# The chunk recurrence of an S5 layer as a hardware tensor scan in a rotated frame, with its rotation table built on GpSimd

## The chip, the core and the metric

The kernel runs on one core of one Trainium2 chip. The core has TensorE (PE, matrix products; PEld loads its weights), VectorE (DVE), ScalarE (ACT), GpSimd (POOL) and SyncE (SP), which run their own instruction queues in order and meet through semaphores; SP, and here POOL too, also issue the DMA transfers. The metric is the device time of one execution in microseconds (us), the median of several runs. A difference of 0.2% is about what a measurement of this kernel can tell from no change.

## The reference, cut to what matters

One inference step of a two-layer decoder: layer 0 mixes tokens with HGRN2, layer 1 with S5, and each layer then has a SwiGLU block and a per-layer embedding. There are 512 prompt tokens and 64 sample tokens (8 sequences of 8), 1024 features, all in 32-bit floats. The S5 mixer is the part that changes:

```python
u = x.astype(f32).reshape(bsz, t, S5_GROUPS, S5_GROUP)          # 64 groups of 16 channels
lam_bar = jnp.exp(lam * delta)                                  # 64 groups x 64 complex states
bu = jnp.einsum('btgc,gpc->btgp', u.astype(jnp.complex64), b_bar)
bu = bu.at[:, 0].add(lam_bar * h0)
_, h = lax.associative_scan(s5_combine, (a_el, bu), axis=1)     # h_t = lam_bar * h_{t-1} + bu_t
y = jnp.einsum('btgp,gcp->btgc', h, c_mat).real + d_skip * u
y = jax.nn.gelu(y.reshape(bsz, t, D_MODEL))
val, gate = jnp.split(y @ w_glu, 2, axis=-1)
return val * jax.nn.sigmoid(gate), h_last.real, h_last.imag
```

## The kernel before

The 576 tokens lie in two blocks of 288 columns. For S5 each block is 36 chunks of 8 tokens: block 0 holds prompt chunks 0 to 27 and the 8 sample chunks, block 1 prompt chunks 28 to 63. Within a chunk everything is a matrix product; from chunk to chunk a complex recurrence runs, `h[k+1] = lam8 * h[k] + z[k]`, for 64 groups by 64 states. A state's real part lies on partitions 0 to 63 and its imaginary part on 64 to 127, so one step of the recurrence (`advance`, L1428) is five VectorE operations: one product, two products that swap the halves (64 partitions each), two sums.

The S5 layer in program order:

1. While layer 0's SwiGLU runs on TensorE, a generator (`s5_prep`, `s5_prep_steps`) computes the layer's coefficient matrices in small steps on VectorE, and sends them to DRAM scratch through POOL's DMA queue (`zw_scratch`, `cl_scratch`, `mg_scratch`). It goes round 18 times; the `zw` tile has a single buffer.
2. `z_part` of block 0: TensorE makes the chunk inputs z, eight groups (an octet) at a time; ScalarE copies them from PSUM into the state tile `HS[0]` (in the trace a tile with the name `xl`).
3. The chunk recurrence of block 0 on VectorE: `many` joins neighbouring chunks in pairs (wide operations), `pair_step` runs the recurrence over the pairs with `lam16` (64-column operations, one chunk pair after the other), `many` fills in the chunks between.
4. `z_part` of block 1 (into `HS[1]`), then `lag_part` for eight octets (the products inside a chunk, for both blocks), then `out_part(0, o)` for eight octets: TensorE applies the output matrices to the states, VectorE adds the result to `u` (the eight `u<-u,mm` operations), ScalarE applies Gelu, and SP sends `y` to DRAM and reads it back as features (`y_load`). The recurrence of block 1 (`last_states`) is a generator whose steps are placed between these octets by the tables `SL` and `SO0`; what is left of it comes later.
5. The GLU products of block 0 for three output tiles, then `out_part(1, o)`, which needs all states of block 1, then the other GLU products.

ScalarE and VectorE take PSUM banks in turn: TensorE has four banks (`mm`) for all of these products, so it goes on only when one has been read.

The weights stream through all of this: each 512 KB slot is loaded raw (`wraw`, two buffers), rounded by ScalarE (`whi`), and the rest is subtracted (`wlo`). During the S5 part that subtraction runs on POOL, otherwise on VectorE.

Of the kernel before, what the change touches and what calls it, by code (L numbers as in the profile page):

```python
# [8 lines left out]
FP32 = mybir.dt.float32  # L9
# [4 lines left out]
OP = mybir.AluOpType  # L14
# [54 lines left out]
OCT = 2  # L69
SL = (0, 1, 1, 1, 1, 1, 1, 0)  # L70
SO0 = (1, 1, 1, 1, 2, 1, 1, 1)
SY0 = (1, 1, 1, 1, 1, 1, 1, 1)
SE = 1
# [69 lines left out]
def hybrid_decoder_kernel(ctx: ExitStack, tc: tile.TileContext, a: dict):  # L143
# [984 lines left out]
    lam8 = const.tile([128, 2, NG], FP32, name="lam8")  # L1128
    lam16 = const.tile([128, 2, NG], FP32, name="lam16")
    ZL = const.tile([128, NG, 9], FP32, name="zl")  # L1130
# [5 lines left out]
    def s5_prep_steps(sp):  # L1136
# [37 lines left out]
        yield  # L1174
        t1 = s64("t1")
        for j in range(2, 9):
# [133 lines left out]

        todo = []
        for i in range(18):
            if 0 < i < 8:
                zeros(i)
            if i < 16:
                load(i)
                yield
            if i >= 2:
                lag_kernels(i - 2)
                if (i - 2) % 8 == 7:  # L1320
                    todo += [((i - 2) // 8, s, j) for s in range(8) for j in range(4)]
                yield
            if 0 < i < 17:
                coeffs(i - 1)
                yield
                inputs(i - 1)
                yield
            for _ in range(4):
                if todo:
                    toeplitz(*todo.pop(0))  # L1330
        while todo:
            toeplitz(*todo.pop(0))
            if len(todo) % 4 == 0:
                yield
# [51 lines left out]
    def z_part(blk, o, zw):  # L1386
# [3 lines left out]
        if blk == 0:  # L1390
            copy(HS[0][:, g, 1:KA], v[:, :, 0:KA - 1])
            copy(HS[1][:, g, 0:1], v[:, :, KA - 1:KA])
# [55 lines left out]

    def many(blk, x0, n, half):

        gs = slice(32 * half, 32 * half + 32)
        w = [t[:, 0:32 * n].rearrange("p (g n) -> p g n", n=n) for t in s5["work"]]
        x, y = (HS[blk][:, gs, i:i + 2 * n - 1:2] for i in (x0, x0 + 1))
        advance(y, x, y, n, w, gs=gs)

    def pair_step(j):
        advance(chunk_state(j + 2), chunk_state(j), chunk_state(j + 2), lam=lam16)

    s5 = {}

    def layer0_to_1():
# [32 lines left out]


        spare = {}
        chunk_tiles("xh", spare, 1)
        spare = spare[1].rearrange("p g k -> p (g k)")
        s5["work"] = [spare[:, T * i:T * i + T] for i in range(2)]
        settle(0)  # L1500
        for b in range(2):
            chunk_tiles("xl", HS, b)
        nc.vector.memset(HS[0][:, :, 0:1], 0.0)


# [52 lines left out]
        def last_states():  # L1558
            for half in range(2):
                many(1, 0, 18, half)  # L1560
                yield
            for j in range(KA - 1, 63, 2):
                pair_step(j)
                if j == KA - 1:
                    advance(chunk_state(KA), chunk_state(j), chunk_state(KA))
                yield
            advance(po, chunk_state(63), ZL[:, :, 8])
            nc.vector.tensor_scalar(po, po, NSG, None, op0=OP.mult)
            nc.gpsimd.dma_start(a["s5o"], po)
            for half in range(2):  # L1570
                many(1, 1, 17, half)
                yield

# [10 lines left out]
        yt = [[spare[:, (4 + o % 4) * NB:(5 + o % 4) * NB] for o in range(8)],  # L1584
              [U[0][:, 8 * o:8 * o + 8].rearrange("p g k -> p (g k)") for o in range(8)]]
        for o in range(8):
# [16 lines left out]
        for o in range(8 - YD, 8):  # L1603
            step(y_loads[0, o])
        tails["scan"] = scan

# [214 lines left out]
```

## Time and profile before

| | before |
|---|---|
| median of 3 runs | 1597.84 us (1597.0 to 1600.13) |
| profiled execution: its own time, its span | 1600.95 us, 1599.1 us |
| mean granted TensorE clock | 0.98 |
| busy: PE, DVE, ACT, POOL | 95%, 59%, 43%, 15% of the span |

All times of the trace are counted from the start of the profiled span. The span is 1.85 us shorter than that execution's own time, and the profiled execution is 3.1 us slower than the median run. TensorE is busy nearly everywhere; its share is low in one place, between about 900 and 1050 us, which is the S5 mixer.

### The profile page before, as it was taken

How to read it: one execution, taken by the hardware profiler on the slowest of the kernel's cores; microseconds unless marked ns; L12 is line 12 of the kernel's file. 1: busy time of each engine (PE TensorE's matmuls, PEld its weight loads, DVE VectorE, ACT ScalarE, POOL GpSimd, SP SyncE). 2: the span in 40 equal slices, each digit the busy share in tenths (PEclk: the TensorE clock that was granted, in tenths of full speed). 3: DMA queues.
4: the chain of work that ended last, by engine and by line, in shares of the span. 5: the costliest groups of instructions: out<-in, count | busy, mean ns of one | idle time of the engine just before them, and what ended most of it. 6: DMA issues, size and time to landing. Idle time of an engine off the chain costs nothing.

```text
span 1599.1 us, 30007 instructions
## 1 busy us (share of the span) xinstructions
PE 1516.2 (95%) x12550; PEld 1468.0 (92%) x12550; DVE 940.2 (59%) x1833; ACT 687.7 (43%) x1159; POOL 238.6 (15%) x284
## 2 busy tenths in 40 slices
PE   8999999889999999999999956799999999999998
PEld 8898989788999999999989956799999999999997
DVE  5748475858557666743486799457533333334685
ACT  5646464736532233123377533336522232133375
POOL 1303020202001112260012432202000000000111
PEclk9999999999999999999999997899999999999999
DMA  5213131242225666753216973332222222223021
GB/s 184 96 67 108 68 109 68 83 126 93 67 70 145 194 191 182 213 153 94 79 67 197 166 280 83 88 106 80 67 80 93 80 80 80 92 80 119 28 79 59
DMA packets 96390, 175.59 MB, mean 110 GB/s; under 512 B 41792, under 2 KB 56816, under 8 KB 96256
## 3 DMA queue, kind: packets, MB, share of 16 engines
q1 hardware_dynamic: 87856, 149.56, 30.7%
q0 software_dynamic: 8400, 24.13, 5.5%
q8 instruction: 98, 1.61, 0.4%
q14 instruction: 36, 0.29, 0.1%
HBM read 148.72 MB, written 24.94 MB: 109 GB/s over the span
## 4 chain that ended last, share of the span: by engine, by line
PE 76%; DVE 14%; ACT 5%; DMA 2%; issue 2%; POOL 1%; SPq 0%; DVEq 0%; ACTq 0%; POOLq 0%
PE mm L299 24%; PE mm L300 23%; PE mm L301 23%; DVE xh L203 2%; DVE wlo L203 1%; DVE xl L203 1%; DVE am L203 1%; DVE b L580 1%; DVE ac L203 1%; DVE xf L203 1%; PE mm L1377 1%; PE tr L709 1%; ACT whi L200 1%; DVE ln_z L203 1%; DVE ln_q L203 1%
## 5 line engine op out<-in xcount | busy, mean ns | idle before, releaser
L299 PE MATMUL mm<-xh,whi 128*128 128x288 f32 x2048 | 611.1, 298 | 7.6 <-ACT xh L200 4.0
L300 PE MATMUL mm<-xl,whi 128*128 128x288 f32 x2048 | 610.2, 298 | 4.5 <-POOL xl L203 3.0
L301 PE MATMUL mm<-xh,wlo 128*128 128x288 f32 x2048 | 607.6, 297 | 1.3 <-DVE wlo L203 1.3
L299 PEld LDWEIGHTS mm<-xh,whi 128*128 128x128 f32 x2048 | 389.0, 190 | 14.0 <-ACT xh L200 5.6
L300 PEld LDWEIGHTS mm<-xl,whi 128*128 128x128 f32 x2048 | 388.9, 190 | 8.1 <-POOL xl L203 4.6
L301 PEld LDWEIGHTS mm<-xh,wlo 128*128 128x128 f32 x2048 | 388.8, 190 | 1.5 <-DVE wlo L203 1.5
L200 ACT ACTIVATE whi<-wraw 128x1024 fp32r<-128x1024 f32 x208 | 218.6, 1053 | 223.1 <-PE mm L300 122.4
L203 DVE TENSOR_TENSOR wlo<-wraw,whi 128x1024 fp32r<-128x1024 f32 x200 | 246.1, 1247 | 29.3 <-ACT whi L200 28.7
L299 PE MATMUL mm<-hhi,whi 128*128 128x288 f32 x704 | 209.6, 298 | 0.0
L301 PE MATMUL mm<-hhi,wlo 128*128 128x288 f32 x704 | 207.8, 295 | 0.0
L300 PE MATMUL mm<-hlo,whi 128*128 128x288 f32 x704 | 207.5, 295 | 0.0
L203 DVE TENSOR_TENSOR fs<-fs,mm 128x288 f32<-128x288 f32 x88 | 40.0, 454 | 267.3 <-PE mm L301 258.2
L299 PEld LDWEIGHTS mm<-hhi,whi 128*128 128x128 f32 x704 | 132.3, 188 | 1.7 <-issue 1.4
L300 PEld LDWEIGHTS mm<-hlo,whi 128*128 128x128 f32 x704 | 132.3, 188 | 0.3
L301 PEld LDWEIGHTS mm<-hhi,wlo 128*128 128x128 f32 x704 | 132.2, 188 | 0.0
L299 PE MATMUL mm<-xhi,whi 128*128 128x320 f32 (+1 forms) x384 | 121.7, 317 | 0.0
L300 PE MATMUL mm<-xlo,whi 128*128 128x320 f32 (+1 forms) x384 | 113.6, 296 | 0.0
L301 PE MATMUL mm<-xhi,wlo 128*128 128x320 f32 (+1 forms) x384 | 113.5, 295 | 0.0
L203 POOL TENSOR_TENSOR ln_s<-ln_s,xf 128x288 f32<-128x288 f32 x24 | 24.3, 1010 | 576.5 <-DVE xf L203 454.9
L200 ACT ACTIVATE hhi<-fs 128x288 fp32r<-128x288 f32 x88 | 38.9, 442 | 149.3 <-DVE fs L203 149.3
L197 ACT ACTIVATE fs<-mm,eps 128x288 f32<-128x288 f32 x88 | 44.1, 501 | 136.0 <-PE mm L301 135.8
L299 PEld LDWEIGHTS mm<-xhi,whi 128*128 128x128 f32 x384 | 72.8, 190 | 6.9 <-issue 4.4
(292 smaller groups left out, 2159.9 us busy)
## 6 DMA issues: line engine op xcount, KB each, us to landing
wraw<-in_w_dram SPq DMA_DIRECT2D x198, 512.0 KB
wraw<-in_w_dram POOLq DMA_DIRECT2D x10, 512.0 KB, 5.2
S<-in_s_dram SPq DMA_DIRECT2D x8, 512.0 KB
out_hgs_dram<-So SPq DMA_DIRECT2D x8, 512.0 KB
wr<-wt_scratch SPq DMA_DIRECT2D x16, 256.0 KB
bT<-in_s5bt_dram SPq DMA_DIRECT2D x16, 256.0 KB
cl_scratch<-cl POOLq DMA_DIRECT2D x16, 256.0 KB, 3.2
zw_scratch<-zw POOLq DMA_DIRECT2D x16, 256.0 KB, 6.2
```

Of the source, the lines that this page charges most:

```text
L197: nc.scalar.activation(out, in_, func, bias=ZERO if bias is None else bias, scale=scale)
L200: nc.scalar.activation(out, in_, ACT.Copy)
L203: (eng or nc.vector).tensor_tensor(out, x, y, op=op)
L299: nc.tensor.matmul(out, whi, rhi, start=start, stop=False)
L300: nc.tensor.matmul(out, whi, rlo, start=False, stop=False)
L301: nc.tensor.matmul(out, wlo, rhi, start=False, stop=stop)
L580: nc.vector.tensor_tensor_scan(b[l], segm[l], L, 0.0, op0=OP.mult, op1=OP.add)
L709: nc.tensor.matmul(ps[s0:s0 + l, o + s0 + l:o + s0 + 2 * l], KL[:, q0:q0 + l], QL[:, q0:q0 + l], start=True, stop=True)
L1377: nc.tensor.matmul(ps[r:r + 64, c], w[:, j, r:r + 64], xo[:, c], start=True, stop=True)
```

## The change

The recurrence is done by VectorE's scan instruction instead of pair by pair. A complex `lam8` is a length `rho` and a direction; if chunk k's input is first turned back by k times that direction, the recurrence in the turned frame has the real factor `rho` alone and real and imaginary parts no longer mix. So for a quarter of the groups (16 of 64) at a time: `turn(..., True)` (four VectorE operations), `run_on` (one scan over 16 x 36 = 576 columns, and one copy that writes the lengths for the next quarter), `turn(..., False)` (four operations). `many`, `pair_step` and `lam16` go.

The turning needs the cosines and sines of k times the angle for k = 0 to 35: a table of 2 x 64 x 36 columns. `s5_prep_steps` gets a generator `table` that makes it on GpSimd by repeated squaring and products, three steps of it in each of the 18 rounds of the preparation, and sends it to DRAM scratch. At the start of the S5 part SP loads it into SBUF, in two transfers (`turn`, and one that takes the memory of block 1's features).

The step tables `SL` and `SO0` change with it, all of the recurrence of block 1 is now issued before the GLU, the first copy out of block 0 fills one column range instead of two, and the sample states `h0` are put into `HS[0]` by ScalarE instead of VectorE.

```diff
-SL = (0, 1, 1, 1, 1, 1, 1, 0)
-SO0 = (1, 1, 1, 1, 2, 1, 1, 1)
+TB = 3
+SL = (0, 0, 1, 0, 1, 0, 1, 0)
+SO0 = (0, 1, 0, 1, 0, 1, 0, 1)
...
+        def square(c, z, c0, z0):
+            tt(ta, z0, z0, OP.mult, P)
+            tt(tb, c0, z0, OP.mult, P)
+            tt(c, c0, c0, OP.mult, P)
+            tt(c, c, ta, OP.subtract, P)
+            tt(z, tb, tb, OP.add, P)
...
+        def turns(half):
+            gs = slice(32 * half, 32 * half + 32)
+            C, Z = (sp.tile([128, 32, 36], FP32, tag=x, name=x) for x in ("tC", "tZ"))
...
+            for m in range(6):
+                n0 = 1 << m
+                n = min(n0, 36 - n0)
...
+                tt(A, c0, bc, OP.mult, P)
+                tt(B, z0, bz, OP.mult, P)
+                tt(c, A, B, OP.subtract, P)
+                yield
+                tt(A, z0, bc, OP.mult, P)
+                tt(B, c0, bz, OP.mult, P)
+                tt(z, A, B, OP.add, P)
+                yield
+            nc.gpsimd.dma_start(tb_d[:, 0, gs], C)
+            P.tensor_scalar(Z, Z, NSG, None, op0=OP.mult)
+            nc.gpsimd.dma_start(tb_d[:, 1, gs], Z)
+            yield
+
+        def table():
+            yield from basis()
+            yield from turns(0)
+            yield from turns(1)
...
         todo = []
+        tabling = table()
         for i in range(18):
...
+            step(tabling, TB)
             for _ in range(4):
                 if todo:
                     toeplitz(*todo.pop(0))
+        run(tabling)
...
-    def many(blk, x0, n, half):
...
-    def pair_step(j):
-        advance(chunk_state(j + 2), chunk_state(j), chunk_state(j + 2), lam=lam16)
+    def turn(blk, q, back):
+
+        gs, n = slice(16 * q, 16 * q + 16), slice(1, 36 if blk else KA + 1)
+        h, c, C, Z = (x[:, n] if len(x.shape) == 2 else x[:, :, n] for x in
+                      (HS[blk][:, gs], s5["c"], s5["C"][:, gs], s5["Z"][:, gs]))
+        tt(c[0:64], h[64:128], Z[64:128], OP.mult)
+        tt(c[64:128], h[0:64], Z[0:64], OP.mult)
+        tt(h, h, C, OP.mult)
+        tt(h, h, c, OP.add if back else OP.subtract)
+
+    def lengths(q):
+        nc.vector.tensor_copy(s5["rho"][:, :, 1:36], rho[:, 16 * q:16 * q + 16, None].to_broadcast([128, 16, 35]))
+
+    def run_on(blk, q):
+        h = HS[blk][:, 16 * q:16 * q + 16].rearrange("p g k -> p (g k)")
+        nc.vector.tensor_tensor_scan(h, s5["rho"].rearrange("p g k -> p (g k)"), h, 0.0, op0=OP.mult, op1=OP.add)
+        lengths((q + 1) % 4)
...
+        for n, x in enumerate((s5["C"], s5["Z"])):
+            nc.sync.dma_start(x.rearrange("p g k -> p (g k)"), tb_d[:, n].rearrange("p g k -> p (g k)"))
...
-        for half in range(2):
-            many(0, 2, KA // 2 - 1, half)
-        for j in range(1, KA - 1, 2):
-            pair_step(j)
-        for half in range(2):
-            many(0, 1, KA // 2 - 1, half)
+        for q in range(4):
+            turn(0, q, True)
+            run_on(0, q)
+            turn(0, q, False)
+        nc.vector.tensor_copy(HS[1][:, :, 0], HS[0][:, :, KA])
...
-        nc.vector.tensor_scalar(HS[0][:, :, KA:36], h0, NSG, None, op0=OP.mult)
+        act(HS[0][:, :, KA:36], h0, ACT.Identity, scale=NSG)
...
         def last_states():
-            for half in range(2):
-                many(1, 0, 18, half)
+            for q in range(4):
+                turn(1, q, True)
+                run_on(1, q)
                 yield
-            for j in range(KA - 1, 63, 2):
-                pair_step(j)
-                if j == KA - 1:
-                    advance(chunk_state(KA), chunk_state(j), chunk_state(KA))
+                turn(1, q, False)
                 yield
...
-        tails["scan"] = scan
+        run(scan)
...
-                    settle("scan")
```

On VectorE, where block 0's recurrence begins, the order of the kernel before is this (`xl_9912` is `HS[0]`, `xh_9911` a work tile, `lam_86` and `lam_87` the factors `lam8` and `lam16`). The first four rows are `many` for half of the groups, the last four one `pair_step`, which comes thirteen times:

```order
L203 TENSOR_TENSOR xh_9911<-xl_9912,lam_86 128x416
L203 TENSOR_TENSOR xh_9911<-xl_9912,lam_86 64x416 x2
L203 TENSOR_TENSOR xh_9911<-xh_9911,xl_9912 128x416
L203 TENSOR_TENSOR xl_9912<-xh_9911 128x32x13
...
L203 TENSOR_TENSOR am<-xl_9912,lam_87 128x64
L203 TENSOR_TENSOR ac<-xl_9912,lam_87 64x64 x2
L203 TENSOR_TENSOR am<-am,xl_9912 128x64
L203 TENSOR_TENSOR xl_9912<-am,ac 128x64
```

In its place stands, for each of four quarters of the groups, the following (`xl_10107` is `HS[0]`, `turn` and `xh_10103` the two halves of the table, `pr_10106` the tile with the work columns and the lengths; the row of L1533 is the scan):

```order
L203 TENSOR_TENSOR pr_10106<-xl_10107,xh_10103 64x16x28 x2
L203 TENSOR_TENSOR xl_10107<-xl_10107,turn 128x16x28
L203 TENSOR_TENSOR xl_10107<-xl_10107,pr_10106 128x16x28
L1533 SCALAR_TENSOR_TENSOR xl_10107<-pr_10106,xl_10107 128x576
L1529 COPY pr_10106<-rho 128x16x35
L203 TENSOR_TENSOR pr_10106<-xl_10107,xh_10103 64x16x28 x2
L203 TENSOR_TENSOR xl_10107<-xl_10107,turn 128x16x28
L203 TENSOR_TENSOR xl_10107<-xl_10107,pr_10106 128x16x28
```

Twenty wide and 65 narrow operations have become 32 wide ones, four scans and four copies; block 1's part changes in the same manner, with 35 columns per group instead of 28.

On ScalarE, just ahead of the copies of block 1's chunk inputs, the row of L197 is new (`xl_10108` is `HS[1]`, `sm` holds the sample states, `pj_10352` the layer's embedding product):

```order
L200 ACTIVATE pj_10352<-mm 128x288 x7
L200 ACTIVATE whi<-wraw 128x1024
L200 ACTIVATE pj_10352<-mm 128x288 x2
L197 ACTIVATE xl_10107<-sm,eps,sgn 128x64x8
L200 ACTIVATE xl_10108<-mm 128x8x35
L200 ACTIVATE zl<-mm 128x8
```

That row writes columns of `HS[0]` that the scans of block 0 run over, so it waits for VectorE's last operation on block 0, and the copies out of PSUM stand behind it in the queue. Before, VectorE wrote these columns itself, after its own last operation on the block.

On POOL, between two rounds of the preparation, there were only DMA issues. This is one of the later rounds, with the piece that now follows its DMA issues (`tC`, `tZ`, `tA`, `tB` are tiles of the table):

```order
L1375 DMA mg_scratch<-zt 1024x1x112
L1339 DMA cl_scratch<-cl 128x4x128
L1353 DMA zw_scratch<-zw 128x512
L203 TENSOR_TENSOR tA<-tZ,pc 128x32x8
L203 TENSOR_TENSOR tB<-tC,pz 128x32x8
L203 TENSOR_TENSOR tZ<-tA,tB 128x32x8
L203 TENSOR_TENSOR tA<-tC,pc 128x512
L203 TENSOR_TENSOR tB<-tZ,pz 128x512
L203 TENSOR_TENSOR tC<-tA,tB 128x32x16
L203 TENSOR_TENSOR tA<-tZ,pc 128x512
```

The next round's DMA of `cl` now stands behind nine table operations.

## Rows read from the trace of the kernel before

**Rows 1.** Waits of PE, 905 to 1050 us: total us, times, longest.

```profile
PE mm L1377 <- DVE u L203: 17.1, 1, 17.1
PE mm L1377 <- DVE gs L203: 7.8, 1, 7.8
```

**Rows 2.** Timeline of DVE in the S5 part: start us, busy us, form, idle before.

```profile
906.95 4.36 DVE L203 TENSOR_TENSOR xh<-xl,lam 128x416 f32<-128x416 f32 x3
911.34 0.59 DVE L203 TENSOR_TENSOR xh<-xh,xl 128x416 f32<-128x416 f32 x1
911.96 0.59 DVE L203 TENSOR_TENSOR xl<-xh 128x416 f32<-128x416 f32 x1
...
945.05 0.48 DVE L1538 TENSOR_SCALAR xl<-sm,sgn 128x512 f32<-128x512 f32 x1
945.45 3.85 DVE L203 TENSOR_TENSOR xh<-xl,lam 128x576 f32<-128x576 f32 x3
...
957.86 0.76 DVE L203 TENSOR_TENSOR xh<-xh,xl 128x576 f32<-128x576 f32 x1
...
974.44 0.83 DVE L203 TENSOR_TENSOR xl<-am,ac 128x64 f32<-128x64 f32 x1
...
981.05 0.44 DVE L203 TENSOR_TENSOR u<-u,mm 128x288 f32<-128x288 f32 x1
...
1008.70 0.45 DVE L203 TENSOR_TENSOR gs<-gs,mm 128x288 f32<-128x288 f32 x1
```

**Rows 3.** Timeline of POOL in the S5 part.

```profile
908.14 2.72 POOL L203 TENSOR_TENSOR wlo<-wraw,whi 128x1024 fp32r<-128x1024 f32 x1
...
945.62 4.60 POOL L203 TENSOR_TENSOR sm<-xl,lam 128x512 f32<-128x512 f32 x3 [21.01 <-DVE xl L1538]
...
974.35 0.79 POOL L203 TENSOR_TENSOR xl<-xh,xh 128x288 fp32r<-128x288 f32 x1 [0.55 <-ACT xh L200]
```

**Rows 4.** Two lines' instructions anywhere: duration in ns, least/median/most.

```profile
L580 DVE TENSOR_TENSOR_SCAN b<-seg,L x32: 1329/1340/1360, 36.0 to 298.7; 128x576 f32<-128x576 bf16 x32
L568 DVE TENSOR_SCALAR e<-e x8: 452/458/463, 32.9 to 291.6; 128x576 f32<-128x576 f32 x8
```

**Rows 5.** Timeline of ACT in the S5 part.

```profile
921.90 0.40 ACT L200 ACTIVATE xl<-mm 128x280 f32<-128x280 f32 x1
922.20 0.18 ACT L200 ACTIVATE zl<-mm 128x8 f32<-128x8 f32 x1
...
972.15 0.80 ACT L197 ACTIVATE sm<-sm,eps,sgn 128x512 f32<-128x512 f32 x1
```

**Rows 6.** Timeline of PE in the S5 part.

```profile
920.73 5.76 PE L1377 MATMUL mm<-u,zw 128*64 128x64 f32 x191 [0.72 <-DMA u<-u_scratch]
...
941.03 2.46 PE L1405 MATMUL mm<-u,zw 128*64 128x72 f32 x70 [2.04 <-issue]
...
981.54 0.61 PE L299 MATMUL mm<-xh,whi 128*128 128x288 f32 x1 [1.13 <-DVE u L203]
...
1001.07 0.29 PE L301 MATMUL mm<-xh,wlo 128*128 128x288 f32 x1
1009.20 9.14 PE L1377 MATMUL mm<-xl,zw 128*64 128x64 f32 x256 [7.83 <-DVE gs L203]
```

**Rows 7.** Timeline of SP's DMA queue at the start of the S5 part.

```profile
894.60 0.79 SPq L1383 DMA_DIRECT2D mg<-mg_scratch  x2
```

**Rows 8.** Busy us of each engine by stretch; then clock, DMA share, GB/s.

```profile
560.00:580.00 20.00, 20.00 (x161) 19.28 (x161) 13.77 (x29) 5.05 (x11) 2.69 (x5) 1.00 0.78 200
...
935.00:940.00 5.00, 3.99 (x126) 3.84 (x122) 4.60 (x16) 3.28 (x8) 0.00 (x0) 1.00 1.03 407
```

**Rows 9.** Timeline of POOL, then of DVE, in one round of the preparation.

```profile
572.33 0.54 POOL L1286 DMA_DIRECT2D zw_scratch<-zw  x1 [5.01 <-DVE zw L206]
...
575.98 0.46 DVE L203 TENSOR_TENSOR fs<-fs,mm 128x288 f32<-128x288 f32 x1 [1.30 <-PE mm L301]
```

**Rows 10.** POOL's issues of `cl`: duration in ns, first and last start us.

```profile
L1272 POOL DMA_DIRECT2D cl_scratch<-cl x16: 757/776/790, 505.8 to 692.9; - x16
```

More of the change, by code (lines that the diff above doesn't have):

```diff
@@ L1128, in hybrid_decoder_kernel @@
     lam8 = const.tile([128, 2, NG], FP32, name="lam8")
-    lam16 = const.tile([128, 2, NG], FP32, name="lam16")
+    rho = const.tile([128, NG], FP32, name="rho")
+    tb_d = nc.dram_tensor("tb_scratch", (128, 2, NG, 36), FP32).ap()
     ZL = const.tile([128, NG, 9], FP32, name="zl")
@@ L1175, in s5_prep_steps, with direction @@
         t1 = s64("t1")
+        P = nc.gpsimd
+        pc, pz = (sp.tile([128, 6, NG], FP32, name=x) for x in ("pc", "pz"))
+        ta, tb = s64("ta"), s64("tb")
+        def square(c, z, c0, z0):
[4 more added lines that the diff above has]
+            tt(z, tb, tb, OP.add, P)
+        def direction(c, z, first):
+            tt(ta, c, c, OP.mult, P)
+            tt(tb, z, z, OP.mult, P)
+            tt(ta, ta, tb, OP.add, P)
+            P.tensor_scalar(tb, ta, -0.5, 1.5, op0=OP.mult, op1=OP.add)
+            tt(c, c, tb, OP.mult, P)
+            tt(z, z, tb, OP.mult, P)
+            if first:
+                P.tensor_scalar(ta, ta, 0.5, 0.5, op0=OP.mult, op1=OP.add)
+                tt(rho, rho, ta, OP.mult, P)
@@ new lines, in s5_prep_steps, with basis @@
+        tt(rho, er, er, OP.mult, P)
+        for _ in range(2):
+            tt(rho, rho, rho, OP.mult, P)
+        square(pc[:, 0], pz[:, 0], r1, r0)
+        def basis():
+            for m in range(8):
+                if m > 1:
+                    direction(pc[:, m - 2], pz[:, m - 2], m == 2)
+                    yield
+                if m < 2:
+                    square(pc[:, 0], pz[:, 0], pc[:, 0], pz[:, 0])
+                elif m < 7:
+                    square(pc[:, m - 1], pz[:, m - 1], pc[:, m - 2], pz[:, m - 2])
+                yield
@@ new lines, in turns @@
+        def turns(half):
+            gs = slice(32 * half, 32 * half + 32)
+            C, Z = (sp.tile([128, 32, 36], FP32, tag=x, name=x) for x in ("tC", "tZ"))
+            P.memset(C[:, :, 0:1], 1.0)
+            P.memset(Z[:, :, 0:1], 0.0)
+            for m in range(6):
+                n0 = 1 << m
+                n = min(n0, 36 - n0)
+                sh = [128, 32, n]
+                bc, bz = (x[:, m, gs, None].to_broadcast(sh) for x in (pc, pz))
+                A, B = (sp.tile([128, 32, 16], FP32, tag=x, name=x)[:, :, 0:n] for x in ("tA", "tB"))
+                c0, z0, c, z = C[:, :, 0:n], Z[:, :, 0:n], C[:, :, n0:n0 + n], Z[:, :, n0:n0 + n]
+                tt(A, c0, bc, OP.mult, P)
[5 more added lines that the diff above has]
+                tt(z, A, B, OP.add, P)
+                yield
+            nc.gpsimd.dma_start(tb_d[:, 0, gs], C)
+            P.tensor_scalar(Z, Z, NSG, None, op0=OP.mult)
+            nc.gpsimd.dma_start(tb_d[:, 1, gs], Z)
+            yield
@@ L1390, in z_part @@
         if blk == 0:
-            copy(HS[0][:, g, 1:KA], v[:, :, 0:KA - 1])
-            copy(HS[1][:, g, 0:1], v[:, :, KA - 1:KA])
+            copy(HS[0][:, g, 1:36], v[:, :, 0:35])
             copy(ZL[:, g, 0:8], v[:, :, KA:36])
@@ L1445, in advance @@
         tt(out, m, c, OP.add, eng)
-    def many(blk, x0, n, half):
[L1451 to L1454, printed above, removed]
-    def pair_step(j):
-        advance(chunk_state(j + 2), chunk_state(j), chunk_state(j + 2), lam=lam16)
+    def turn(blk, q, back):
[12 more added lines that the diff above has]
+        lengths((q + 1) % 4)
     s5 = {}
@@ L1493, in layer0_to_1 @@
         mg, cl = [octet(op, mg_d, o, "mg", OCT) for o in range(OCT)], []
[L1496 to L1499, printed above, removed]
+        s5["C"] = op.tile([128, NG, 36], FP32, name="turn")
+        turn_z = {}
+        chunk_tiles("xh", turn_z, 1)
+        s5["Z"] = turn_z[1]
+        for n, x in enumerate((s5["C"], s5["Z"])):
+            nc.sync.dma_start(x.rearrange("p g k -> p (g k)"), tb_d[:, n].rearrange("p g k -> p (g k)"))
+        s5["rho"], s5["c"] = (x for x in s5["zp"].tile([128, 2, 16, 36], FP32, tag="praw", name="pr2").rearrange(
+            "p n g k -> n p g k"))
         settle(0)
@@ L1503, in layer0_to_1 @@
         nc.vector.memset(HS[0][:, :, 0:1], 0.0)
+        nc.vector.memset(s5["rho"][:, :, 0:1], 0.0)
+        lengths(0)
         for o in range(8):
@@ L1569, in last_states @@
             nc.gpsimd.dma_start(a["s5o"], po)
-            for half in range(2):
-                many(1, 1, 17, half)
-                yield
+            yield
         scan = last_states()
@@ L1582, in y_start @@
                 step(y_loads[b, o - 2])
-        yt = [[spare[:, (4 + o % 4) * NB:(5 + o % 4) * NB] for o in range(8)],
-              [U[0][:, 8 * o:8 * o + 8].rearrange("p g k -> p (g k)") for o in range(8)]]
+        yt = [[U[0][:, 8 * o:8 * o + 8].rearrange("p g k -> p (g k)") for o in range(8)]] * 2
         for o in range(8):
```

5 lines of the change are left out of this document (removed).

## The prediction

> **What bounds the kernel now.** I looked first for the place where TensorE waits. In nearly the whole program it is full: in the stretch of the preparation it is busy 20.00 of 20 us [rows 8]. In the S5 part two waits stand out, 17.1 us for a `u` of VectorE and 7.8 us for a `gs` of VectorE [rows 1]; the reader is to see that both releasers are VectorE. Its own timeline then shows why: from 906.95 to 1008.70 it is never idle, since no row carries an idle time [rows 2]. It does block 0's recurrence (906.95 to 945.05), then block 1's, with the eight `u` additions in between, the last at 981.05. So VectorE's queue sets the S5 part, and two of its moments count for TensorE: the last `u`, which frees the bank with which the GLU products start (the PE row of 981.54 waits for it), and the end of block 1's recurrence, for which `out_part(1)` waits from 1001.36 to 1009.20 [rows 6]. From there on the same program follows in both kernels, so what start `out_part(1)` gains, the end gains.
>
> **Prices.** A 416-column operation starts 0.62 us after the one before it (911.34 to 911.96), a 576-column one costs 0.76 and a gap of 0.03 [rows 2]. By columns, that makes 0.66 for block 0's turns (16 x 28 = 448) and 0.77 for block 1's (560). The scan is an instruction that the trace has: 1.34 us for 576 columns [rows 4]. Its first operand there is narrower than the change's; I see nothing that makes a wider one cheaper, and above I bound it by twice that, 2.7, which for eight scans would be 11 us. The nearest row is the same form, so 1.34. The copy of the lengths has no row; a one-input operation on 576 columns takes 0.46 [rows 4], a two-input one 0.76 [rows 2], and I take 0.46 (the other end costs 2.4 us over eight).
>
> **Block 0.** A quarter is 8 x 0.66 + 1.34 + 0.46 = 7.1 us, four are 28.4. POOL's `wlo` pieces stop VectorE: three operations that should take 1.86 us took 4.36 at 906.95, while POOL ran a `wlo` of 2.72 from 908.14 [rows 2, 3]. Three such pieces fall into block 0 and all three stay, about 6 us. With 0.3 for the new column copy, block 0 ends at 906.95 + 28.4 + 6 + 0.3 = 941.7, against 945.45 before (the 0.48 operation of 945.05 goes to ScalarE).
>
> **The moved operation.** ScalarE's write of the sample states now waits for 941.7, and block 1's copies out of PSUM stand behind it. It takes 0.80, like the row of the same size, and then VectorE needs two octets' copies, 0.48 each [rows 5]: block 1 can begin at 943.5, with 1.8 us of VectorE idle. Before, these copies began at 921.90, hidden under block 0. TensorE is pushed back too: octets 4 to 7 wait for banks. An octet of these products takes 0.96 us (32 instructions at 5.76/191) [rows 6]. Four octets from about 943 end at 947, `lag_part`'s eight at 954.7, and three gaps of some 2.05 us like the one ahead of 941.03 [rows 6], and the first octet of `out_part(0)`, make 962.
>
> **Block 1 up to the last `u`.** By the new tables, VectorE does quarter 0 and the forward half of quarter 1 ahead of the first `u`: 12 x 0.77 + 2 x 1.8 = 12.9 us. POOL's sample work (4.60 us for its first three operations [rows 3], more behind) collides as before: the eight operations from 945.45 to 957.86 needed 12.4 us where 6.2 would do [rows 2], so 6.2 us again. That gives 962.6, level with TensorE's 962. Then eight `u` at 0.48 and three halves (3.1, 4.9, 3.1) are 14.9, and three collisions with POOL's 0.79 us pieces [rows 3] at 0.55 (0.83 instead of 0.28 at 974.44 [rows 2]) are 1.6: the last `u` ends at 979.1, where it ended at 981.5.
>
> **The rest.** The GLU products took from 981.54 to 1001.36 [rows 6], 19.8 us; now they end at 998.9. VectorE needs after 979.1 one forward half, one back half, 1.8 us for the last state and some 2.7 us of collisions: 991.6. That is 7 us ahead of TensorE, so the 7.8 us wait goes and `out_part(1)` starts at 998.9 instead of 1009.20: a gain of 10.3 us.
>
> **What it costs elsewhere.** (a) The table must have landed by 906.95. Its two transfers are 2 x 1.18 MB and are issued behind the two `mg` of 0.5 MB at 894.60 [rows 7]. At 407 GB/s, which long rows reach here [rows 8], 3.4 MB take 8.4 us: 903. At half that, 911.4, a loss of 4.5 us. I take 1 us. The small writes of `u` are queued behind and land later, but block 1's octets now wait for ScalarE until 943 and cover it. (b) The table's making: 153 POOL operations on 18,600 columns. At the 3.0 ns per column of the 512-column row (4.60/3) [rows 3] this is 56 us; if every operation under 288 columns cost the 0.79 of that row, 130 us. I take 80, since the narrow ones must cost less than the 288-column one. It is spread over 14 rounds of 12.5 us (16 issues from 505.8 to 692.9) [rows 10]. The cover is VectorE's slack: 13.77 of 20 us busy [rows 8], and an `fs` that came as soon as TensorE had finished, after 1.30 us of idling [rows 9]. A piece starts when `zw` has been issued (572.33), just as VectorE begins its two `wlo`. A late `fs` hurts only when all four banks are full. I take 1 us of TensorE waits in sum, in the two rounds with 512-column pieces. If the cover is gone, see the third rival. (c) The removed `lam16` work and the simpler copies of block 0: nothing, they lie under full engines' waits.
>
> The sum is -10.3 + 1 + 1 = -8.3. The profiled execution took 1600.95 and would take 1592.6; the median run is 3.1 faster, so 1597.84 - 8.3 = 1589.5, say 1590.
>
> **A rule weighed against this.** The Trainium skill (SBUF — State Buffer, Who interferes with whom) says that a VectorE instruction with two SBUF inputs and a GpSimd instruction that reads SBUF cannot run at once, and the later one waits for all of the other. The collision at 906.95 agrees: 2.5 us lost to a 2.72 us piece. By that rule nothing of the table is free once VectorE's and POOL's shares exceed the time; by my reading most of it falls into VectorE's idle time. The rule's result is the third rival.
>
> **Rivals.**
> - *The S5 part gains only half* (chance 0.25). The table lands late (4.5 us), or TensorE, pushed back by ScalarE's wait, delivers the first `u` 4 us late. For it speaks that TensorE's 962 is level with VectorE's 962.6, with nothing to spare; against it, that the transfers have 12 us. Gain 4 to 5: 1593.5.
> - *It gains more* (0.10): the collisions with the sample work shrink, since longer operations collide less often. VectorE's half of 6.2 us: 1586, if TensorE keeps up.
> - *The table slows the SwiGLU* (0.15; the other side). VectorE is busy 69% of the preparation, and 80 us in 175 are 46%: together 115%. What exceeds the time, 0.15 x 175 = 26 us, would reach TensorE through late `fs` and `wlo`: 1597.8 - 10 + 26 = 1614. It decides from about 12 us of TensorE waits on, that is from POOL pieces at 70 us if none fell into idle time. Against it: the additions that read PSUM and VectorE's waits leave gaps, and POOL's pieces come right where VectorE waits for TensorE.
> - *The recurrence is off the path* (0.05): `out_part(1)` is held by something else, as a weight slot on POOL, which now comes behind the last state's DMA. No change: 1598.
>
> **How the numbers follow.** The forecast, 1586.5 to 1592.5, has 0.45. Faster than 1594.6 (0.2%) are the forecast, the larger gain, and two thirds of the half gain: 0.72. Within 0.2% are the rest of the half gain, the last rival and a little of the third: 0.15. Slower: 0.13. The range 1585 to 1600 leaves out most of the third rival and some of the larger gain.
>
> **What would show it.** Right: a scan of 1.3 us eight times; VectorE's first turn at 907; its block 1 at 943 to 944; no TensorE wait ahead of `out_part(1)`, which starts near 999; TensorE full from 500 to 700. Wrong: an idle VectorE at 907 that waits for a DMA; TensorE waits for `fs` or `wlo` in the preparation; scans of more than 2 us; a first `u` well behind 963.

## The result, and the profile after

| | before | changed |
|---|---|---|
| median of 5 runs each | 1599.72 us (1597.0 to 1600.93) | 1589.6 us (1586.45 to 1593.91) |
| profiled execution, its span | 1600.95, 1599.1 us | 1589.6, 1587.8 us |
| ratio | 1 | 0.9943, 95% interval 0.9922 to 0.9965 |

The change makes the kernel faster, by 10.1 us between the medians and by 11.3 us between the two profiled executions. The forecast was 1590, a gain of 8.3 us.

The waits of TensorE first: view of waits, 905 to 1050 us, columns as in [rows 1].

```profile
PE mm L1447 <- ACT zl L200: 12.1, 1, 12.1
PE mm L1447 <- DMA u<-u_scratch: 8.2, 1, 8.2
...
PE mm L299 <- ACT gs L197: 1.5, 1, 1.5
```

The two waits of [rows 1], 17.1 and 7.8 us, are gone. Two that look as large have come in their place, but they lie earlier, while VectorE is still at block 0. VectorE's timeline in the S5 part (start us, busy us, form, idle before) shows how little of them reaches it, an idle time of 1.58 us ahead of block 1:

```profile
909.65 2.08 DVE L203 TENSOR_TENSOR pr<-xl,xh 64x448 f32<-64x448 f32 x2 [2.25 <-DMA xh<-tb_scratch]
911.83 0.63 DVE L203 TENSOR_TENSOR xl<-xl,turn 128x448 f32<-128x448 f32 x1
...
913.15 3.43 DVE L1533 TENSOR_TENSOR_SCAN xl<-pr,xl 128x576 f32<-128x576 f32 x1
...
924.33 1.36 DVE L1533 TENSOR_TENSOR_SCAN xl<-pr,xl 128x576 f32<-128x576 f32 x1
925.73 0.45 DVE L1529 COPY pr<-rho 128x560 f32<-128x560 f32 x1
...
943.22 0.23 DVE L1599 COPY xl<-xl 128x64 f32<-128x64 f32 x1
945.02 2.60 DVE L203 TENSOR_TENSOR pr<-xl,xh 64x560 f32<-64x560 f32 x2 [1.58 <-ACT xl L200]
...
953.19 2.44 DVE L1529 COPY pr<-rho 128x560 f32<-128x560 f32 x1
...
963.62 0.45 DVE L203 TENSOR_TENSOR u<-u,mm 128x288 f32<-128x288 f32 x1
...
978.61 0.81 DVE L203 TENSOR_TENSOR u<-u,mm 128x288 f32<-128x288 f32 x2
...
990.40 0.27 DVE L203 TENSOR_TENSOR am<-xl,lam 128x64 f32<-128x64 f32 x1
```

Read against [rows 2], the reader sees block 0 end at 943.45 (before: 945.53 with the samples' write), block 1 begin at 945.02 (945.45), the last `u` end at 979.42 (981.49) and the recurrence end at 990.4 (the row of 990.40 is the step for the last state), where the recurrence of block 1 had run until just ahead of 1008.70. Two rows are odd: the first scan takes 3.43 us and the copy at 953.19 takes 2.44. POOL's timeline has the reason, a `wlo` beside each:

```profile
912.90 2.46 POOL L203 TENSOR_TENSOR wlo<-wraw,whi 128x1024 fp32r<-128x1024 f32 x1 [1.42 <-ACT whi L200]
...
951.90 3.42 POOL L203 TENSOR_TENSOR wlo<-wraw,whi 128x1024 fp32r<-128x1024 f32 x1
```

TensorE's timeline, to be read against [rows 6]:

```profile
926.75 5.94 PE L1447 MATMUL mm<-u,zw 128*64 128x64 f32 x128 [8.19 <-DMA u<-u_scratch]
944.76 5.51 PE L1447 MATMUL mm<-u,zw 128*64 128x64 f32 x128 [12.07 <-ACT zl L200]
...
964.17 7.58 PE L1447 MATMUL mm<-xl,zw 128*64 128x64 f32 x201 [3.03 <-issue]
...
979.11 0.61 PE L299 MATMUL mm<-xh,whi 128*128 128x288 f32 x1 [1.43 <-DVE u L203]
...
994.32 0.40 PE L299 MATMUL mm<-xh,whi 128*128 128x288 f32 x1 [1.52 <-ACT gs L197]
...
1000.86 7.66 PE L1447 MATMUL mm<-xl,zw 128*64 128x64 f32 x256
```

`out_part(1)` starts at 1000.86 instead of 1009.20, without a wait, and it takes 7.66 us instead of 9.14. The 8.3 us in its start are made up of 2.4 us by which the GLU products start earlier (979.11 instead of 981.54) and the 7.8 us of the wait, less 1.9 us by which the products take longer. No run keeps the old step tables with the scan, so how much of this comes from the scan and how much from the new order is not shown.

To set the kernels of this study side by side, the table below takes three moments of each profiled execution: the first z product of block 0, the start of `out_part(1)`, and the matrix product of layer 1's next norm that takes `ln_q`. (The moments of before are 894.23, 1009.20 and 1086.45, those of after 895.01, 1000.86 and 1075.35.) The norm lies behind the whole change; from there to the end every kernel but the last takes 512 to 513 us, and the last 514.5.

| kernel | z to `out_part(1)` | to the norm | sum, us | ratio to before | interval |
|---|---|---|---|---|---|
| before | 114.97 | 77.25 | 192.2 | 1 | |
| changed | 105.85 | 74.49 | 180.3 | 0.9943 | 0.9922 to 0.9965 |
| change_again | 105.81 | 75.34 | 181.2 | 0.9932 | 0.9913 to 0.9950 |
| h0_on_vector | 104.51 | 75.21 | 179.7 | 0.9928 | 0.9911 to 0.9944 |
| table_first | 104.62 | 74.50 | 179.1 | 0.9926 | 0.9912 to 0.9940 |
| no_table_work | 106.85 | 75.64 | 182.5 | 0.9932 | 0.9919 to 0.9946 |
| ring_early | 104.69 | 75.90 | 180.6 | 0.9938 | 0.9923 to 0.9953 |
| before_filled | 115.10 | 72.91 | 188.0 | 0.9995 | 0.9984 to 1.0005 |
| u_first | 91.64 | 84.18 | 175.8 | 0.9877 | 0.9861 to 0.9893 |
| u_first_queue | 92.28 | 82.72 | 175.0 | 0.9903 | 0.9888 to 0.9919 |
| u_first_samples | 90.90 | 82.56 | 173.5 | 0.9907 | 0.9891 to 0.9924 |
| reordered_again | 95.03 | 82.18 | 177.2 | 0.9912 | 0.9893 to 0.9930 |
| reordered_filled | 92.81 | 81.67 | 174.5 | 0.9894 | 0.9877 to 0.9911 |

change_again is the changed kernel once more, and reordered_again is u_first_samples once more; their pairs tell how far one profiled execution of the same kernel lies from another, 0.8 us and 3.7 us in the sum. A difference of about 1 us between two rows is thus within what a repeat shows.

### The profile page after: what moved, and what is told of

Read it like the earlier page. It is cut to its first block, busy times and chain, and to the rows that moved or that the text cites. A ratio compares the mean times of both kernels' runs of the same rounds, so it can differ in the third digit from the quotient of the medians.

```text
span 1587.8 us, 30040 instructions
## 1 busy us (share of the span) xinstructions
PE 1514.9 (95%) x12550; PEld 1467.1 (92%) x12550; DVE 947.1 (60%) x1711; ACT 687.9 (43%) x1152; POOL 342.9 (22%) x447
## 5 line engine op out<-in xcount | busy, mean ns | idle before, releaser
L197 ACT ACTIVATE fs<-mm,eps 128x288 f32<-128x288 f32 x88 | 44.1, 502 | 131.0 <-PE mm L301 130.9
```

The source lines that it names most:

```text
L197: nc.scalar.activation(out, in_, func, bias=ZERO if bias is None else bias, scale=scale)
```

## The experiments

The theory behind the first four is that of the prediction: VectorE's queue sets the S5 part, TensorE's pushed-back products and the table cost little. The rivals are that ScalarE's wait, the table's landing or the table's making takes a good part of the gain.

**h0_on_vector** undoes one line of the change:

```diff
-        act(HS[0][:, :, KA:36], h0, ACT.Identity, scale=NSG)
+        nc.vector.tensor_scalar(HS[0][:, :, KA:36], h0, NSG, None, op0=OP.mult)
```

> The changed kernel with one part undone: VectorE writes the sample states into HS[0] again, so ScalarE no longer waits for the end of block 0. Theory (the place of the u additions in VectorE's queue sets TensorE): VectorE begins block 1 at 943.9 instead of 945.0 and the last u comes about 1 us earlier; TensorE gets through its lag products before 950 but then waits some 12 us for the first u; ScalarE's and TensorE's own waits vanish without gain. Time 1 us less than the changed kernel at most, ratio to before 0.993 to 0.995. Rival (TensorE, pushed back by ScalarE's wait, sets the first u): the last u moves up by 3 us or more, ratio 0.992 or less.

TensorE's timeline: `out_part(0)` is ready early and then waits for VectorE.

```profile
953.90 2.30 PE L1447 MATMUL mm<-xl,zw 128*64 128x64 f32 x73 [0.29 <-issue]
964.21 3.64 PE L1447 MATMUL mm<-xl,zw 128*64 128x64 f32 x64 [8.01 <-DVE u L203]
```

The 12.1 us wait for ScalarE is gone, and an 8.0 us wait for a `u` stands there instead. Counted from the first z product, the first `u` comes 0.6 us earlier than before the edit (68.0 instead of 68.6) and `out_part(1)` 1.3 us. So ScalarE's place in the queue held up TensorE for 12 us and cost about one; the rival, 3 us or more, is out.

**table_first** moves the two `mg` transfers behind the table's:

```diff
-        mg, cl = [octet(op, mg_d, o, "mg", OCT) for o in range(OCT)], []
...
             nc.sync.dma_start(x.rearrange("p g k -> p (g k)"), tb_d[:, n].rearrange("p g k -> p (g k)"))
+        mg, cl = [octet(op, mg_d, o, "mg", OCT) for o in range(OCT)], []
```

> The changed kernel with its two table transfers issued ahead of the two mg transfers. Theory (the table lands late because 3.4 MB share the DMA engines): the table lands about 2 us earlier, VectorE's first turn starts at 907.5 instead of 909.65, block 0 ends 2 us earlier and everything up to out_part(1) moves by 2 us: ratio 0.993. Rival (the loads wait for something else, as the memory or the rows being written): the first turn stays at 909.6 and the time is the same, 0.9943.

VectorE's timeline:

```profile
906.79 1.77 DVE L203 TENSOR_TENSOR pr<-xl,xh 64x448 f32<-64x448 f32 x2
908.65 2.65 DVE L203 TENSOR_TENSOR xl<-xl,turn 128x448 f32<-128x448 f32 x1
...
912.00 1.36 DVE L1533 TENSOR_TENSOR_SCAN xl<-pr,xl 128x576 f32<-128x576 f32 x1
```

The first turn starts without an idle time, so it was the order of the transfers that made the table late. Counted from the first z product, the first turn starts 2.2 us earlier (12.4 instead of 14.6). Of this, 0.6 us reach the end of block 0 (47.9 instead of 48.4) and 1.2 us `out_part(1)`, where 2 were expected: a collision now stretches another operation, the one of 908.65. The time moves with it in direction, less than the runs can tell.

**no_table_work** takes 147 of the table's operations off POOL and fills the table with two memsets per half, which leaves the rotation out:

```diff
-            P.memset(C[:, :, 0:1], 1.0)
-            P.memset(Z[:, :, 0:1], 0.0)
-            for m in range(6):
...
+            P.memset(C, 1.0)
+            P.memset(Z, 0.0)
...
-            yield from basis()
```

> The changed kernel without the making of the table: GpSimd fills it with ones and zeros and sends it out in the same places (this leaves the rotation out). Theory (the 100 us of GpSimd work fall into VectorE's slack): VectorE's busy time in 490 to 700 us goes back from 169 to about 147 us, TensorE stays full and the time is the changed kernel's, ratio 0.993 to 0.9955. Rival (the table slows the SwiGLU without showing as a wait of TensorE): at least 4 us faster than the changed kernel, ratio 0.9915 or less.

Busy time of each engine in 490 to 700 us (columns as in [rows 8]): before, then changed, then no_table_work.

```profile
490.00:700.00 210.00, 209.27 (x1644) 203.29 (x1643) 146.03 (x332) 53.32 (x85) 46.72 (x77) 1.00 0.66 187
```

```profile
490.00:700.00 210.00, 209.92 (x1648) 203.91 (x1647) 168.63 (x330) 53.39 (x85) 147.25 (x232) 1.00 0.73 199
```

```profile
490.00:700.00 210.00, 209.86 (x1647) 203.81 (x1646) 145.69 (x329) 53.00 (x85) 53.17 (x86) 1.00 0.68 199
```

The table costs POOL 100.5 us (147.25 - 46.72) and VectorE 22.6 us of longer operations, and TensorE nothing: it is busy for 209.9 of 210 us with the table and without it. The ratio is the changed kernel's. The third rival of the prediction is out.

**u_first** asks what VectorE's order costs. In the changed kernel the recurrence ends at 990.4 and has no successor until 1000.86, while the GLU waits for the last `u`. Here the sample states are written by VectorE, the table is loaded ahead of `mg`, the `u` additions follow block 1's first quarter, and the rest of the recurrence runs beside the GLU products:

```diff
-SL = (0, 0, 1, 0, 1, 0, 1, 0)
-SO0 = (0, 1, 0, 1, 0, 1, 0, 1)
+SL = (1, 0, 0, 0, 0, 0, 0, 0)
+SO0 = (0, 0, 0, 1, 0, 0, 0, 1)
+SG = (3, 1, 1)
...
-        run(scan)
+        step(scan, SG[0])
...
                 if (blk, m) == (0, 3):
+                    run(scan)
...
+                if blk == 0 and m < 2:
+                    step(scan, SG[m + 1])
```

Since the table's memory is then in use until `out_part(1)`, one of the three further weight slots is put where `mg` was, the other two are opened at `out_part(1)`, and the first `gs` tiles take the memory of `h0`.

> The changed kernel with VectorE's queue put in another order: the sample states written by VectorE, the table ahead of mg, the eight u additions right behind block 1's first quarter, and the rest of the recurrence beside the GLU products of block 0 (which need a ring of weights opened in two steps). Theory (VectorE's order, not its load, delays the GLU; the recurrence has about 8 us to spare): last u near 955 instead of 979.4, GLU from about 958 to 978, out_part(1) at 982 to 988 when the recurrence ends, instead of 1000.9; time 12 to 17 us below the changed kernel, ratio 0.984 to 0.987. Rival (the u additions were not what held the GLU; the round trip of y through DRAM or the weights do): out_part(1) later than 994, ratio 0.990 or more.

Waits of TensorE, 960 to 1015 us:

```profile
PE mm L300 <- DVE xl L204: 3.5, 1, 3.5
PE mm L1448 <- DVE gs L204: 3.0, 2, 1.7
...
PE mm L1448 <- DVE u L204: 1.7, 2, 1.3
```

The last `u` ends at 958.93 (near 955 was expected) and `out_part(1)` starts at 984.69, as expected. The time does not follow in full: 0.9877, 9 to 11 us below the changed kernel by the ratios and not 12 to 17. `out_part(1)` now begins before the recurrence has ended (octets 0 to 5 need three quarters only) and then waits in between for `gs` and `u`, 4.7 us in sum. From there to the norm it takes 84.2 us instead of 74.5. One row over this stretch (length, busy us of PE, PEld, DVE, ACT and POOL, granted clock, DMA share, GB/s), to be read against the row of the changed kernel under before_filled:

```profile
984.69:1068.87 84.18, 76.81 (x719) 72.96 (x718) 44.73 (x86) 32.21 (x53) 6.15 (x8) 0.94 0.33 92
```

TensorE idles 7.4 us instead of 2.0, and is busy for 76.8 us instead of 72.5 with the same products, at a mean granted clock of 0.94 instead of 0.98.

**u_first_queue** leaves the weights on POOL's queue until `out_part(1)` has been issued, so that two loads of 512 KB no longer stand among SyncE's transfers of `y`:

```diff
-                    st.update(queue=nc.sync, lo=nc.vector, load=LOAD_MM, split=SPLIT_MM)
                     for n in range(8):
                         out_part(1, n, cl[n])
...
+                    st.update(queue=nc.sync, lo=nc.vector, load=LOAD_MM, split=SPLIT_MM)
```

> The reordered kernel (u_first) with the weights' loads and low parts left on GpSimd until out_part(1) has been issued; there, two loads of 512 KB stood between the y stores and y loads in SyncE's queue, and TensorE waited for features between 1006 and 1012. Theory (these loads delay the round trip of y): features of block 1 arrive 2 to 3 us earlier, TensorE's idle time at 1005 to 1012 shrinks, time 2 to 4 us below u_first: ratio 0.985 to 0.9865. Rival (the DMA engines, not the queue, are the limit there): no change, 0.9877.

From the start of `out_part(1)` to the last feature of block 1 it took 26.6 us (991.44 to 1018.03) where u_first took 27.9 (984.69 to 1012.59), so in these two executions the loads cost 1.3 us and not 2 to 3. The time did not improve (0.9903 against 0.9877, on another chip). The theory was wrong in size, and the run gives no gain.

**u_first_samples** is u_first_queue with the step of the sample sequences on VectorE:

```diff
-SE = 1
+SE = 0
```

> The kernel of u_first_queue with the sample sequences' last step on VectorE instead of GpSimd. Theory (a GpSimd operation beside VectorE's costs VectorE more than doing it itself: 6.2 us of collisions against five operations of 0.7 us): VectorE's recurrence ends 2 to 3 us earlier although it has 3.4 us more to do; out_part(1), which waits for VectorE's gs and u, ends 1.5 to 3 us earlier; ratio 0.9835 to 0.9855. Rival (VectorE's added work counts in full and the collisions only move to other GpSimd operations): 1 to 3 us slower than u_first_queue.

VectorE's timeline has the five operations:

```profile
948.16 2.10 DVE L204 TENSOR_TENSOR sm<-xl,lam 128x512 f32<-128x512 f32 x3
950.29 0.69 DVE L204 TENSOR_TENSOR sm<-sm,zl 128x512 f32<-128x512 f32 x1
951.02 0.69 DVE L204 TENSOR_TENSOR sm<-sm 128x512 f32<-128x512 f32 x1
```

They take 3.5 us. From the start of block 1's recurrence to its last state it took 47.1 us (943.32 to 990.43); in u_first_queue, with POOL doing this work, it was 48.1 (949.16 to 997.24). Although VectorE does 3.5 us more, the stretch is 1.0 us shorter and not 2 to 3. The same kernel once more (reordered_again, below) took 49.7 (945.52 to 995.19), so a gain is not shown; what is shown is that the collisions with POOL cost VectorE about as much as the work. In the section this is 1.5 us (173.5 against 175.0), in the time nothing that can be told (0.9907 against 0.9903).

**ring_early** is the changed kernel with one of the three further weight slots in the memory of `mg`:

```diff
+        mo_pool.close()
         for o in range(8):
             out_part(0, o, cl[o])
...
+        ring = work.enter_context(more_weights(1, (p0 + 128) // 8, "ext2"))
         op_pool.close()
         outer.close()
...
-        with more_weights(WX, (p0 + 128) // 8):
+        with more_weights(WX - 1, (p0 + 128) // 8):
```

> The changed kernel with one of the three further weight slots put where the mg tiles were, which is free after lag_part, instead of where the table and the work columns are. Theory (ScalarE's whi at 990.45, and with it the gs for which TensorE waited 1.5 us, was held because its slot lies in the table's memory, which VectorE reads until 990.36): the first of the two whi runs at 987.3, the second at 990.4, gs at 992.7 instead of 993.8, TensorE's wait for gs shrinks from 1.5 to about 0.5 us and out_part(1) starts 1 us earlier, near 999.9. Rival (the whi waits for something else that ends then): whi again at 990.4 and out_part(1) at 1000.9.

ScalarE's timeline in the changed kernel:

```profile
990.45 2.01 ACT L200 ACTIVATE whi<-wraw 128x1024 fp32r<-128x1024 f32 x2 [3.11 <-DVE xl L203]
...
993.77 0.89 ACT L197 ACTIVATE gs<-mm,eps 128x288 f32<-128x288 f32 x2
```

And with the earlier slot:

```profile
987.74 1.04 ACT L200 ACTIVATE whi<-wraw 128x1024 fp32r<-128x1024 f32 x1
990.32 1.06 ACT L200 ACTIVATE whi<-wraw 128x1024 fp32r<-128x1024 f32 x1 [1.54 <-issue]
...
992.69 0.90 ACT L197 ACTIVATE gs<-mm,eps 128x288 f32<-128x288 f32 x2
```

The first `whi` no longer waits for VectorE's last turn, `gs` comes 1.1 us earlier, TensorE's wait for it falls from 1.5 to 0.4 us and `out_part(1)` starts 1.1 us earlier. The new wait of the changed kernel is thus the weight slot in the table's memory. To the norm nothing is left of it (180.6 us against 180.3), and the ratio, 0.9938, is the changed kernel's.

**before_filled** adds work to the kernel before. Between the GLU products and `out_part(1)` TensorE multiplies into a spare bank that nobody reads:

```diff
                 if (blk, m) == (0, 3):
+                    ps = tr_bank()
+                    for j in range(18):
+                        hi, lo = w_ap(p0 + 32 + j % 8)
+                        mm3(ps[:, :NB], hi, lo, x_hi(j % 8, 0), x_lo(j % 8, 0), j == 0, j == 17)
                     settle("scan")
```

> The kernel before with one thing added: 54 matmuls of the GLU's form (128x288) into a spare PSUM bank, which nobody reads, between the GLU products and out_part(1), so that TensorE computes through most of the 7.8 us in which it waited for VectorE. Theory (a part of the change's gain, 2.8 us between out_part(1) and 1086 us, is TensorE's granted clock, which was 0.50 for 3.4 us after that wait): out_part(1) still starts at about 1009.2 but takes 7.7 us instead of 9.14; the stretch at 0.50 behind 1030 stays, or gets shorter; time 1.5 to 2.8 us less than before, ratio 0.998 to 0.999, although work was added. Rival (the shorter out_part(1) after the change has another cause, as data that arrive sooner): out_part(1) takes 9.1 us and the time is the same or longer.

Windows of the kernel before (the third figure from the right is the granted clock; 0.50 is 1.2 GHz, 1.00 is 2.4 GHz):

```profile
1009.20:1012.00 2.80, 2.80 (x52) 2.80 (x54) 2.45 (x6) 0.25 (x1) 0.00 (x0) 0.50 0.03 6
...
1027.00:1030.00 3.00, 2.32 (x9) 1.31 (x9) 0.46 (x1) 1.42 (x4) 0.82 (x2) 0.93 0.56 88
1030.00:1032.00 2.00, 1.74 (x6) 1.42 (x7) 0.27 (x1) 1.69 (x2) 0.76 (x1) 0.50 0.00 0
...
1034.00:1036.00 2.00, 2.00 (x10) 2.00 (x9) 0.00 (x0) 0.00 (x0) 0.00 (x0) 0.50 0.00 0
```

And of before_filled, with its row of `out_part(1)` from TensorE's timeline behind them:

```profile
1010.80:1012.00 1.20, 1.20 (x41) 1.20 (x43) 1.17 (x4) 0.00 (x0) 0.00 (x0) 1.00 0.00 0
...
1027.00:1030.00 3.00, 2.26 (x10) 1.36 (x9) 0.71 (x2) 1.67 (x4) 1.07 (x2) 1.00 0.43 68
1030.00:1032.00 2.00, 1.53 (x12) 1.43 (x12) 0.47 (x2) 1.45 (x2) 0.52 (x1) 1.00 0.00 0
...
1034.00:1036.00 2.00, 2.00 (x16) 1.89 (x15) 0.46 (x1) 0.68 (x2) 0.00 (x0) 1.00 0.00 0
```

```profile
1010.78 7.66 PE L1377 MATMUL mm<-xl,zw 128*64 128x64 f32 x256
```

With work in the place of the wait, `out_part(1)` takes 7.66 us as in the changed kernel, and the second stretch at 0.50, from 1030 on, is gone too. From `out_part(1)` to the norm it took 72.9 us instead of 77.3. The rows over this whole stretch, of before, the changed kernel and before_filled:

```profile
1009.20:1086.45 77.25, 75.80 (x718) 73.29 (x718) 36.83 (x72) 28.90 (x49) 5.59 (x7) 0.93 0.31 86
```

```profile
1000.86:1075.35 74.49, 72.47 (x720) 70.41 (x719) 36.26 (x69) 30.68 (x51) 8.02 (x9) 0.98 0.37 102
```

```profile
1010.78:1083.69 72.91, 71.15 (x719) 69.10 (x719) 36.95 (x72) 28.94 (x49) 5.60 (x7) 1.00 0.33 91
```

For the same products TensorE is busy 75.8 us at a mean granted clock of 0.93, 72.5 at 0.98 and 71.2 at 1.00, while its idle time stays between 1.5 and 2.0 us. The median of the 12 executions is only 0.05% lower than that of before, and the interval (0.9984 to 1.0005) holds no change as well as the 1.5 us of the first stretch. So that the clock is the cause of the shorter `out_part(1)`, and of the shorter way to the norm, is shown in these profiled executions; that it is worth 4 us in every run is not.

**change_again, reordered_again and reordered_filled** ran on one chip. The third adds to the second idle matmuls behind `out_part(0)` and behind the GLU's fourth output tile:

```diff
+        ps = tr_bank()
+        for _ in range(9):
+            nc.tensor.matmul(ps[:, :160], ones[512], cst, start=True, stop=True)
         y_start(0, 8)
...
+                    ps = tr_bank()
+                    for j in range(6):
+                        hi, lo = w_ap(p + j)
+                        mm3(ps[:, :NB], hi, lo, x_hi(j, 0), x_lo(j, 0), j == 0, j == 5)
                     for n in range(KD):
                         step(y_loads[1, n])
```

> The changed kernel itself, on the chip on which the two reordered kernels run, so that these can be set against it. Expected by every theory: ratio to before 0.993 to 0.995; from the start of block 0's z products to layer 1's first norm about 180 us, where the kernel before took 192.

> The kernel of u_first_samples once more, beside the changed kernel on one chip. Theory (VectorE's order and its collisions cost the changed kernel some 7 us more between the z products and the norm, 173.5 against 180.3): 6 to 8 us faster than the changed kernel, ratio to before 0.988 to 0.990. Rival (the 173.5 of that one profiled execution is chance, and 0.9907 is all there is): within 3 us of the changed kernel.

> The reordered kernel with idle matmuls added, whose results nobody reads, in the two waits behind which TensorE's granted clock was 0.50 (nine of 128x160 behind out_part(0), eighteen of 128x288 behind the GLU's fourth output tile). Theory (the clock falls after such a wait and gives back some 3 us at the first place and 2.5 at the second; the first is hidden by VectorE): no stretch at 0.50 behind 1003 us, the norm 1 to 3 us earlier, ratio 0.001 to 0.002 below that of the reordered kernel. Rival (in runs without a profile this hardly shows, as with the filled kernel before, whose time changed by 0.05%): the same ratio within 0.001.

Windows of reordered_again, then of reordered_filled:

```profile
1014.00:1018.00 4.00, 2.59 (x13) 1.57 (x11) 0.73 (x2) 2.26 (x4) 1.60 (x2) 0.87 0.51 79
1018.00:1025.00 7.00, 7.00 (x43) 6.89 (x44) 1.83 (x4) 2.05 (x5) 0.00 (x0) 0.83 0.00 0
```

```profile
1014.00:1018.00 4.00, 3.32 (x23) 3.10 (x24) 1.83 (x4) 2.36 (x4) 1.20 (x2) 1.00 0.00 0
1018.00:1025.00 7.00, 7.00 (x53) 6.89 (x53) 3.43 (x10) 4.09 (x7) 0.00 (x0) 1.00 0.01 2
```

The medians are 1589.03, 1585.54 and 1582.66 us. Of the 6 to 8 us that were expected of the new order, 3.5 came in this round, and its interval overlaps the changed kernel's; the 173.5 us of the one earlier execution were a favourable one of that kernel. The filled version has no low clock there and is another 2.9 us lower in median, again within the intervals. What can be said is that every reordered kernel had a lower ratio than every run of the changed one (0.9877 to 0.9912 against 0.9932 and 0.9943), by 3 to 11 us; which of them is best is not settled.

## Why the prediction was right

**Prices.** All three held where no POOL operation ran beside: a block 0 turn at 0.66 from start to start (911.83 to 912.49), the scan at 1.36 against 1.34 although its first operand is a wide f32 one, and the copy of lengths at 0.45 against 0.46. The fear that the scan could cost twice as much by its wide operand had no ground. But the sign "a scan of 1.3 us eight times" came true for five only: POOL's pieces stretched the others, two of them to 3.43 and 2.32 us.

**Block 0.** From the first turn to the column copy it took 33.6 us, 28.4 of them by the prices, so 5.2 us of collisions where 6 were taken. The end was 1.7 us later than forecast since the start was 2.7 us late: the step **(a)** had the table at 903 or, at half the rate, 911.4; it came at 909.65. So one sign of being wrong was there, an idle VectorE at 907 that waits for a DMA, and it cost little: table_first puts it at 1.2 us at `out_part(1)`, against the 1 us taken.

**The moved operation and block 1.** VectorE idled 1.58 us (1.8 forecast), block 1 began at 945.02 (943.5), the first `u` at 963.62 (962.6), the last `u` ended at 979.42 (979.1). TensorE was pushed back by 12 us and still delivered the first octet in time; the late `u` transfers (8.2 us) lay wholly under ScalarE's wait, as step (a) had said. By h0_on_vector the wait for ScalarE cost 1.3 us. The recurrence, with the last state, ended at 992.1 (991.6).

**The GLU.** Here a step was off: the 19.8 us were taken over from before, but the products took 21.75 (979.11 to 1000.86), and `out_part(1)` started 1.9 us later than the 998.9 forecast. 1.5 us of this is TensorE's wait for `gs`, and ring_early shows its cause: a `whi` whose slot lies in the memory of the table stood ahead of `gs` in ScalarE's queue and waited for VectorE's last turn. The prediction had asked what is late next for TensorE and VectorE, and not who gets the memory of the new tiles.

**What `out_part(1)` gains, the end gains.** This sentence of the first part failed. `out_part(1)` gained 8.3 us (1009.20 to 1000.86), the norm behind it 11.1. The other 2.8 us are TensorE's granted clock, a term that the prediction did not have: after the 7.8 us wait the kernel before ran at 0.50 for some 3.3 us, and again for about 7 us around 1030 to 1036, where the changed kernel has some 3.4 us (0.50 in 1020 to 1022, 0.66 in 1022 to 1024). before_filled shows it, with the three rows of that stretch. The misses have opposite signs, 1.9 us of GLU products against 2.8 us of clock and the 1 us under (b) that did not come, so the sum of -8.3 stands beside -11.3 in the profiled execution and -10.1 in the medians. That 1590 and 1589.6 lie so close is luck besides: the five runs of before have a median 1.9 us above the 1597.84 from which the forecast counted.

**The table's making.** (b) took 80 us of POOL within bounds of 56 and 130; it was 100.5. Of this 6.4 us are two operations on 1152 columns each that its count of 153 on 18,600 columns leaves out. The 1 us of TensorE waits was none. The rule of the Trainium skill (SBUF — State Buffer, Who interferes with whom), by which one of the two engines waits for the whole instruction of the other, is borne out in single rows: the scan of 913.15, beside a `wlo` with 2.21 us still to run, took 2.07 us longer. The third rival made of it a loss as soon as both shares exceed the time. They did (146 and 100 of 210 us, 117%), and nothing was lost: VectorE's operations became only 22.6 us longer by POOL's 100.5, and VectorE had 64 us of idle time for that.

The half gain had spoken of a late table of 4.5 us or a first `u` 4 us late; table_first puts the former at 1.2 us, and the first `u` came 1.0 us late (963.62 against 962.6). The larger gain (1586, a gain of 11.8) lies about as near to the measured 10.1 as the forecast's 8.3 does, but its mechanism, fewer collisions, is not what brought the time; block 0 lost 5.2 us to them where 6 were taken.

## What to carry to other kernels

When a wait of TensorE goes away, look at the granted clock behind it: the work that follows may be running at the lower level, as it did here, and may get shorter as well. When new tiles take memory, ask who had it next in the kernel before, and what stands in the queue behind that. And the place of a result in a busy engine's queue can matter more than the load: eight additions put ahead of most of a recurrence, with the table loaded first and the sample states written by VectorE, brought `out_part(1)` 11 to 15 us closer to the z products in five profiled executions, though 7 to 10 us of that were lost again behind it.

## What the runs showed of the hardware that was not expected

- A one-input copy on VectorE was held by GpSimd as well: 2.44 us instead of 0.45, beside a `wlo` of 3.42.
- GpSimd's narrow operations were dear: between 490 and 700 us the 78 two-input ones on 64 columns took 0.50 us each in the mean, 7.8 ns per column, and the 12 on 512 columns 1.37 us, 2.7 ns per column, waits for VectorE included in both.
- The clock did not fall when TensorE's wait was filled with matmuls that nobody reads (1.00 through the stretch that had been at 0.50), and the 7 us of low clock from 1030 on were gone too in that execution, although the pauses ahead of them were still there (2.32 of 3 us busy at 1027 before, 2.26 with the filling).
